# Hybrid attention/Mamba layer on one core: index queries of three token blocks instead of four, and four products for the decay sums instead of fifteen

## The chip, the core and the metric

The kernel runs on one core of a Trainium2 chip. That core has a matrix engine (TensorE, PE in the profile, with its weight loads shown apart as PEld), VectorE (DVE), ScalarE (ACT), GpSimd (POOL) and SyncE (SP), which issues most transfers. The metric is the device time of one execution in microseconds; the kernel before takes 1356.84 us, the median of three runs (1355.81 to 1357.34).

## The reference

One layer is computed for 512 new tokens of one stream (positions 0 to 511, no past) and for 64 tokens of another (positions 512 to 575, with 512 cached keys). Width 1024, everything float32. Cut to what bears on the change:

```python
h = rms_normalize(x) * g_norm_mix * (1.0 + sc1) + sh1
q, k, v, qi, ki, wi, z, xbc, dt, gate_logits = split(h @ w_in)
qi = rope(qi.reshape(b, t, 8, 64), pos); ki = rope(ki, pos)        # index queries, index keys
# per block of 128 queries:
logits = einsum('thd,sd->ths', qi, ki) * 64 ** -0.5
score = einsum('th,ths->ts', wi, relu(logits))
limit = (pos // 64 + 1) * 64
score = where(kpos < limit, score, -inf)
_, idx = top_k(score, k)            # k = 128 for the 512 tokens, 144 for the 64 (of 576 keys)
valid = idx < limit                 # keys past the limit count for nothing
o = softmax(q . k[idx]) @ v[idx]    # 16 heads, 4 key/value heads
# Mamba-2 branch:
dtp = softplus(dt + dt_bias)                      # 32 heads
acs = cumsum(dtp * -exp(a_log)) within a chunk
decay = exp(where(causal, acs_i - acs_j, -inf))   # chunked scan of xs, bm, cm
y = ssd_scan(...) + d_skip * xs, gated by silu(z), group norm
# merge of both branches by sigmoid gates, output projection, residual, SwiGLU FFN
```

The first 128 tokens of the prompt have at most 128 keys before their limit, so the top 128 are all of them: which keys such a query may read follows from its position alone.

## The kernel before, in words

**The order.** The program records every operation of every engine on paper (class `Plan`, one `Op` each) and then makes one list of all of them (`order`): it simulates the engines with a table of costs and latencies, lets the engine that can start earliest go next, and takes on that engine, of the operations that the simulation holds ready, the one recorded first (`R.prio(n)` lets an operation count as recorded n places earlier; `R.slack` holds a product back by so many us in the simulation). `emit` (line 544) then issues them, so every instruction in the trace carries L544, and groups are told apart by the names of their tiles. Any change of what is recorded makes this list anew, for the whole program.

**Products.** Weights come from HBM as `raw` tiles of 1024 columns; ScalarE rounds them to `wh`, VectorE makes the remainder `wl`. The layer's normed input stands transposed as `hTh` + `hTl` (and `hsS` for the 64 tokens). Each exact product is three: high with high, high with low, low with high. Two pools of PSUM accumulators matter: `mm`, two slots of two banks, for the wide products, and `px` and `py`, two banks each, for transposes, scores and sums.

**Stages.** (1) The input's norm and the small columns (`misc`: index keys, head weights, dt). (2) The index queries `qi`, in two halves of 256 columns (4 heads each): `tm` makes token-major products for four blocks of 128 tokens and for the 64 tokens, into `mm`; ScalarE moves them to `tok`, `rope` rotates them (two products into `tmpb` on VectorE, one on GpSimd, a sum on VectorE), and `q_stack` transposes them on PE and splits them into `qis` (high on ScalarE, low on VectorE). (3) The decay sums: from `dA` (5 chunks x 32 heads) the running sum in a chunk (`tri`), the total (`ones`), and the running sum with heads on rows, which goes through `acsT` to DRAM (`acs_d`). They are products of float32 operands. (4) Scores of blocks 4 (the 64 tokens), 1, 2, 3 and the choice of the top keys by `max` and `match_replace` on VectorE; the results are `mask1` to `mask4`. `mask0` is set by its position alone. (5) Attention for each of the four key/value heads `kv`: score products into `py`, `lg` on VectorE, `P` by ScalarE's exponential, then for each tile of 128 keys a transpose into `px`, a copy `pth` on ScalarE, the remainder `ptl` on VectorE, and two products with the values `vst` into `py`; `otmp` (ScalarE) moves out half of the sum. Two `pth` and two `ptl` buffers alternate. (6) The scan: inputs `xc` from `mm` by ScalarE, convolution `cu`, chunks that load their decay sums as `bc`. (7) Merge and FFN.

**Fillers.** 32 blocks of 128 gate columns are independent of attention and are used as work for PE between its dependent steps. A table says after which stage each block is recorded (`FILL = [5, 5, 5, 4]` for the four `kv`, 1 each for two places in the scan, 11 ahead of attention); the planner takes them when nothing recorded earlier is ready. The scan's input products (`mm<-hTh,wh` and so on, 128x288) are recorded behind attention's last `kv` and serve the same way. Their weights are split in the order of the table. `R.close(at2, ap_)` ends attention's buffers; the scan's tiles come after it.

## Time and profile before

| | before |
|---|---|
| median of three runs | 1356.84 us (1355.81 to 1357.34) |
| the profiled execution's own time | not listed apart; its span is 1353.9 us |
| PE busy | 1341.1 us of the span |
| VectorE busy | 1138.9 us |
| ScalarE busy | 756.7 us |
| GpSimd busy | 247.9 us |
| stages, read from the trace | queries and sums 60 to 125 us, top keys to 239, attention 243 to 452, scan from 452, FFN from about 950 |

A row of the profile names the line, the engine, the operation and its output and input tiles with the shape (partitions x elements), "x4" for four instructions, and in brackets how long the engine was idle just before and which instruction released it. PE's matmuls overlap, so the time from one start to the next says more than the duration of one. The trace of a product with two float32 operands shows two records for one product.

### The profile page before, as it was taken

How to read it: one execution, taken by the hardware profiler on the slowest of the kernel's cores; microseconds unless marked ns; L12 is line 12 of the kernel's file. 1: busy time of each engine (PE TensorE's matmuls, PEld its weight loads, DVE VectorE, ACT ScalarE, POOL GpSimd, SP SyncE). 2: the span in 40 equal slices, each digit the busy share in tenths (PEclk: the TensorE clock that was granted, in tenths of full speed). 3: DMA queues.
4: the chain of work that ended last, by engine and by line, in shares of the span. 5: the costliest groups of instructions: out<-in, count | busy, mean ns of one | idle time of the engine just before them, and what ended most of it. 6: DMA issues, size and time to landing. Idle time of an engine off the chain costs nothing.

```text
span 1353.9 us, 27909 instructions
## 1 busy us (share of the span) xinstructions
PE 1341.1 (99%) x10677; PEld 1307.3 (97%) x10677; DVE 1138.9 (84%) x2303; ACT 756.7 (56%) x1597; POOL 247.9 (18%) x381
## 2 busy tenths in 40 slices
PE   8999999999999999999999999999999999999998
PEld 6999999999999999999999999999999999999998
DVE  5788999887777788888887688867799999878997
ACT  5445343787777666666565342225576666665453
POOL 2312011230301234545463300002100000000000
PEclk9999999999999999999999999999999999999999
DMA  9762435574754464454445688747533343324352
GB/s 300 228 182 82 112 107 155 126 184 108 170 139 119 139 177 112 116 151 129 133 122 172 216 290 256 232 139 250 153 94 94 99 129 102 94 78 138 98 163 64
DMA packets 268454, 201.35 MB, mean 149 GB/s; under 512 B 25553, under 2 KB 239681, under 8 KB 268321
## 3 DMA queue, kind: packets, MB, share of 16 engines
q1 hardware_dynamic: 263056, 183.40, 46.2%
q0 software_dynamic: 4976, 16.05, 5.9%
q8 instruction: 83, 1.36, 0.4%
q14 instruction: 51, 0.41, 0.1%
q10 hardware_dynamic: 288, 0.13, 0.0%
HBM read 157.75 MB, written 28.96 MB: 138 GB/s over the span
## 4 chain that ended last, share of the span: by engine, by line
PE 93%; DVE 4%; issue 1%; ACT 1%; DMA 0%; POOL 0%; DVEq 0%; POOLq 0%; ACTq 0%
PE mm L544 64%; PE py L544 17%; PE px L544 12%; DVE score L544 1%; DVE m L544 1%; DVE wl L544 0%; DMA B<-in_w_down 0%; DVE tok L544 0%; DVE xs L544 0%; DVE rr L544 0%; ACT wh L544 0%; ACT wl L544 0%; POOL tok L544 0%; DVE xn L544 0%; DVE kst L544 0%
## 5 line engine op out<-in xcount | busy, mean ns | idle before, releaser
L544 ACT ACTIVATE wh<-raw 128x1024 fp32r<-128x1024 f32 (+3 forms) x144 | 140.5, 979 | 170.5 <-PE mm L544 133.0
L544 PE MATMUL mm<-hTl,wh 128*128 128x288 f32 (+1 forms) x1024 | 232.7, 302 | 0.9 <-DVE hTl L544 0.9
L544 PE MATMUL mm<-hTh,wh 128*128 128x288 f32 (+1 forms) x1024 | 231.6, 303 | 0.6 <-ACT wh L544 0.5
L544 PE MATMUL mm<-hTh,wl 128*128 128x288 f32 (+1 forms) x1024 | 230.3, 302 | 0.0
L544 PEld LDWEIGHTS mm<-hTl,wh 128*128 128x128 f32 (+1 forms) x1024 | 166.9, 189 | 3.7 <-DVE hTl L544 1.4
L544 PEld LDWEIGHTS mm<-hTh,wh 128*128 128x128 f32 (+1 forms) x1024 | 166.0, 189 | 4.0 <-ACT hTh L544 1.0
L544 PEld LDWEIGHTS mm<-hTh,wl 128*128 128x128 f32 (+1 forms) x1024 | 165.8, 189 | 1.8 <-issue 0.7
L544 DVE TENSOR_TENSOR wl<-raw,wh 128x1024 fp32r<-128x1024 f32 (+2 forms) x99 | 120.9, 1223 | 25.5 <-ACT wh L544 24.3
L544 POOL DMA_DIRECT2D wl<-raw x24 | 22.1, 919 | 472.2 <-PE px L544 313.8
L544 DVE SCALAR_TENSOR_TENSOR cu<-xc,wc,cu 128x579 f32<-128x579 f32 x96 | 83.8, 873 | 2.0 <-ACT cu L544 1.0
L544 PE MATMUL mm<-wh,hTl 128*128 128x256 f32 x256 | 73.2, 286 | 0.0
L544 PE MATMUL mm<-wl,hTh 128*128 128x256 f32 x256 | 72.5, 284 | 0.0
L544 PE MATMUL mm<-wh,hTh 128*128 128x256 f32 x256 | 72.4, 285 | 0.0
L544 DVE SCALAR_TENSOR_TENSOR aacc<-adr,sil,aacc 128x512 f32<-128x512 f32 x84 | 59.1, 753 | 5.0 <-DMA adr<-in_w_ada 4.7
L544 PE MATMUL mm<-yh,wl 128*128 128x288 f32 x256 | 55.2, 296 | 0.0
L544 PE MATMUL mm<-yh,wh 128*128 128x288 f32 x256 | 55.0, 296 | 0.0
L544 PE MATMUL mm<-yl,wh 128*128 128x288 f32 x256 | 54.9, 296 | 0.0
L544 PE MATMUL mm<-xhS,wh 128*128 128x290 f32 (+1 forms) x248 | 54.8, 296 | 0.0
L544 ACT ACTIVATE P<-lg,mn 128x128 f32<-128x128 f32 (+4 forms) x72 | 41.7, 580 | 23.1 <-DVE mn L544 22.0
L544 PE MATMUL mm<-xhS,wl 128*128 128x290 f32 (+1 forms) x232 | 51.2, 296 | 0.0
L544 ACT ACTIVATE dec<-dec,nacs 128x128 f32<-128x128 f32 x128 | 42.4, 392 | 14.4 <-POOL dec L544 14.4
L544 PEld LDWEIGHTS mm<-wh,hTl 128*128 128x128 f32 x256 | 48.3, 189 | 0.4
(569 smaller groups left out, 4077.9 us busy)
## 6 DMA issues: line engine op xcount, KB each, us to landing
raw<-in_w_in SPq DMA_DIRECT2D x80, 512.0 KB, 4.2
adr<-in_w_ada SPq DMA_DIRECT2D x36, 512.0 KB, 5.5
raw<-in_w_gate_up SPq DMA_DIRECT2D x22, 512.0 KB, 3.8
wl<-raw POOLq DMA_DIRECT2D x21, 512.0 KB, 4.9
rawu<-in_w_gate_up SPq DMA_DIRECT2D x20, 512.0 KB, 3.8
bc<-acs_d SPq DMA_DIRECT2D x32, 256.0 KB, 3.5
raw<-in_w_branch_ssm SPq DMA_DIRECT2D x16, 512.0 KB, 4.8
gate_d<-sg SPq DMA_DIRECT2D x16, 288.0 KB, 2.4
```

Of the source, the lines that this page charges most:

```text
L544: getattr(engines[x.eng], x.fn)(*[real(a) for a in x.args], **{k: real(v) for k, v in x.kw.items()})
```

## The change

Two parts, both ahead of attention. First, `tm`, `rope` and `q_stack` take an argument `first`, the first block of tokens that they treat, and the two calls for the index queries pass 1: nothing is made for the first 128 tokens, whose columns of `qis` are read by no score. Each half issues 24 fewer products of 256 columns and 2 fewer transposes; the moves out of `mm`, the four steps of the rotation and the splits into `qis` are shorter. Second, the decay sums of the five chunks are made in one product of 160 columns with `tri`, one with `ones`, one transposed product for the first four chunks (their 4 x 32 rows side by side) and one for the fifth; `acsT` and `acs_d` take that form, are stored in two parts on SP, and the chunks' loads (`bc`) read rows 32c + 4g of it.

```diff
-    def tm(name, tiles, n, out):
+    def tm(name, tiles, n, out, first=0):
         for pr in range(2):
             ps = pmm(f"{name}p{pr}")
-            for j in range(2):
+            j0 = max(first - 2 * pr, 0)
+            for j in range(j0, 2):
...
-                act.activation(out[:, 2 * pr:2 * pr + 2, :], ps[:, :, :n], AF.Copy)
+                act.activation(out[:, 2 * pr + j0:2 * pr + 2, :], ps[:, j0:, :n], AF.Copy)
...
-    def rope(name, x, tab, h, rms):
-        x4 = x.rearrange("p t (h d) -> p t h d", h=h)
-        b = ap_.tile([P, 5, h, HD], F32, name=name + "rb", tag="tmpb", bufs=1)
+    def rope(name, x, tab, h, rms, first=0):
+        x4 = x.rearrange("p t (h d) -> p t h d", h=h)[:, first:]
+        tab = tab[:, first:]
+        nb = 5 - first
+        b = ap_.tile([P, 5, h, HD], F32, name=name + "rb", tag="tmpb", bufs=1)[:, first:]
...
-    def q_stack(st, name, x, pair, h0, n_h):
+    def q_stack(st, name, x, pair, h0, n_h, first=0):
...
-        for tb in range(4):
+        f0 = P * first
+        for tb in range(first, 4):
             pe.transpose(p[:, tb * P:(tb + 1) * P], x[:, tb, P * pair:P * pair + P], ident)
...
-            for src, c0, n in ((p, (h0 + i) * NP_, NP_), (p2, n_h * NP_ + (h0 + i) * NS, NS)):
+            for src, c0, n in ((p[:, f0:], (h0 + i) * NP_ + f0, NP_ - f0), (p2, n_h * NP_ + (h0 + i) * NS, NS)):
...
-        tm(f"qi{hf}", getw(), 256, x)
-        ropes.append(rope(f"qi{hf}", x, cs2, 4, False))
+        tm(f"qi{hf}", getw(), 256, x, 1)
+        ropes.append(rope(f"qi{hf}", x, cs2, 4, False, 1))
         for pr in range(2):
-            q_stack(qis, f"qis{hf}{pr}", x, pr, 4 * hf + 2 * pr, 8)
+            q_stack(qis, f"qis{hf}{pr}", x, pr, 4 * hf + 2 * pr, 8, 1)
...
-    for c in range(5):
-        pe.matmul(p[:, 32 * c:32 * c + 32], tri, dA[:, c, :], start=True, stop=True)
-        pe.matmul(p2[:, 32 * c:32 * c + 32], ones, dA[:, c, :], start=True, stop=True)
+    pe.matmul(p[:, :160], tri, fl(dA), start=True, stop=True)
+    pe.matmul(p2[:, :160], ones, fl(dA), start=True, stop=True)
...
-    p = [px("pacsTa"), px("pacsTb", "py")]
-    for c in range(5):
-        o, i0 = (p[0][:32, P * c:P * c + P], P) if c < 4 else (p[1][:32, :NS], NS)
-        pe.matmul(o, dA[:i0, c, :], tri[:i0, :i0], start=True, stop=True)
+    p = px("pacsT")
+    pe.matmul(p[:, 0:P], fl(dA)[:, 0:P], tri, start=True, stop=True)
+    pe.matmul(p[:32, P:P + NS], dA[:NS, 4, :], tri[:NS, :NS], start=True, stop=True)
...
-    acs_d = R.dram([32, T], F32, name="acs_d")
-    sync.dma_start(acs_d, acsT)
+    acs_d = R.dram([160, P], F32, name="acs_d")
+    sync.dma_start(acs_d[0:P], acsT[:, 0:P])
+    sync.dma_start(acs_d[P:160, 0:NS], acsT[:32, P:])
...
-        sync.dma_start(bc[:, :, :L], acs_d[4 * g:4 * g + 4, i0:i0 + L][None].to_broadcast([P, 4, L]))
+        sync.dma_start(bc[:, :, :L], acs_d[32 * c + 4 * g:32 * c + 4 * g + 4, 0:L][None].to_broadcast([P, 4, L]))
```

The list of operations is made anew, and moves in places far from these lines. Three of them follow. On PE, the end of attention: the last tiles of keys of the last head group before (`ident,P` is a transpose of probabilities, `pth,vst` and `ptl,vst` the products with the values, `mm` a product of the fillers or of the scan's inputs):

```order
L544 MATMUL py_111<-ptl_2725,vst_2708 128x512
L544 MATMUL px_113<-ident_70,P_2720 128x128
L544 MATMUL px_113<-ident_70,P_2721 128x128
L544 MATMUL px_113<-ident_70,P_2722 128x128
L544 MATMUL mm_114<-hTh_126,wl_104 128x288
L544 MATMUL mm_114<-hTh_126,wh_101 128x288 x2
L544 MATMUL mm_114<-hTl_127,wh_101 128x288 x2
L544 MATMUL mm_114<-hTh_126,wl_104 128x288 x2
L544 MATMUL mm_114<-hTh_126,wh_101 128x288 x2
L544 MATMUL mm_114<-hTl_127,wh_101 128x288
L544 MATMUL py_111<-pth_2724,vst_2708 128x512
```

and the same place in the new order:

```order
L544 MATMUL px_112<-ident_70,P_2724 128x128
L544 MATMUL px_113<-ident_70,P_2721 128x128
L544 MATMUL px_113<-ident_70,P_2722 128x128
L544 MATMUL px_113<-ident_70,P_2723 128x128
L544 MATMUL px_113<-ident_70,P_2724 128x128
L544 MATMUL py_110<-pth_2725,vst_2710 128x512
L544 MATMUL py_110<-ptl_2727,vst_2710 128x512
L544 MATMUL py_110<-pth_2726,vst_2710 128x512
L544 MATMUL py_110<-ptl_2728,vst_2710 128x512
L544 MATMUL mm_115<-hTh_126,wh_102 128x288 x2
```

The ten `mm` products between the last transposes and their use have gone from there. On ScalarE, the same place before (`xc` are the scan's inputs, moved out of the `mm` slots):

```order
L544 ACTIVATE pth_2724<-px_113 128x512
L544 ACTIVATE pth_2723<-px_112 128x512
L544 ACTIVATE pth_2724<-px_113 128x512
L544 ACTIVATE otmp_2727<-py_111 64x512
L544 ACTIVATE xc_5110<-mm_115 128x288
L544 ACTIVATE xc_5110<-mm_115 128x224
L544 ACTIVATE xc_5110<-mm_115 128x64
L544 ACTIVATE cu_5112<-xc_5110,bconv_79,wc_78 128x579
L544 ACTIVATE wh_101<-raw_100 128x1024
```

and now:

```order
L544 ACTIVATE pth_2726<-px_113 128x512
L544 ACTIVATE pth_2725<-px_112 128x512
L544 ACTIVATE pth_2726<-px_113 128x512
L544 ACTIVATE otmp_2729<-py_110 64x512
L544 ACTIVATE xc_5056<-mm_115 128x288
L544 ACTIVATE xc_5056<-mm_115 128x224
L544 ACTIVATE xc_5056<-mm_115 128x64
L544 ACTIVATE xc_5057<-mm_114 128x288
L544 ACTIVATE xc_5057<-mm_114 128x224
```

Both `mm` slots now hold inputs of the scan when attention ends; before, one did. On PE, the transposes of the first half's rotated index queries stood among the products of the 64 tokens (hsS):

```order
L544 MATMUL mm_114<-wl_106,hsS_128 128x256
L544 MATMUL mm_114<-wh_101,hsS_128 128x256
L544 MATMUL mm_114<-wl_104,hsS_128 128x256
L544 MATMUL py_110<-ident_70,tok_682 128x128
L544 MATMUL px_113<-ident_70,tok_682 128x128 x4
L544 MATMUL mm_114<-wh_101,hsS_128 128x256
```

and in the new order stand among products with hTh and hTl, 39 rows nearer to the program's start:

```order
L544 MATMUL mm_115<-wh_102,hTh_126 128x256
L544 MATMUL mm_115<-wl_105,hTh_126 128x256
L544 MATMUL mm_115<-wh_102,hTl_127 128x256
L544 MATMUL py_110<-ident_70,tok_682 128x128
L544 MATMUL px_113<-ident_70,tok_682 128x128 x3
L544 MATMUL mm_115<-wh_102,hTh_126 128x256
```

The 39 rows are counted from the first instruction of PE.

More of the change, by code (lines that the diff above doesn't have):

```diff
@@ L1022, in rope @@
             vec.tensor_tensor(x4, x4, r[:, :, :, None].to_broadcast([P, 5, h, HD]), OP.mult)
-        vec.tensor_tensor(b[..., 0:32], x4[..., 32:64], tab[:, :, None, 64:96].to_broadcast([P, 5, h, 32]), OP.mult)
-        vec.tensor_tensor(b[..., 32:64], x4[..., 0:32], tab[:, :, None, 96:128].to_broadcast([P, 5, h, 32]), OP.mult)
-        pool.tensor_tensor(x4, x4, tab[:, :, None, 0:64].to_broadcast([P, 5, h, HD]), OP.mult)
+        vec.tensor_tensor(b[..., 0:32], x4[..., 32:64], tab[:, :, None, 64:96].to_broadcast([P, nb, h, 32]), OP.mult)
+        vec.tensor_tensor(b[..., 32:64], x4[..., 0:32], tab[:, :, None, 96:128].to_broadcast([P, nb, h, 32]), OP.mult)
+        pool.tensor_tensor(x4, x4, tab[:, :, None, 0:64].to_broadcast([P, nb, h, HD]), OP.mult)
         return vec.tensor_tensor(x4, x4, b, OP.add)
@@ L1175, in build @@
     vec.tensor_tensor(wst, wst, dtp, OP.mult)
-    p = [px("pacsTa"), px("pacsTb", "py")]
-    for c in range(5):
-        o, i0 = (p[0][:32, P * c:P * c + P], P) if c < 4 else (p[1][:32, :NS], NS)
-        pe.matmul(o, dA[:i0, c, :], tri[:i0, :i0], start=True, stop=True)
+    p = px("pacsT")
+    pe.matmul(p[:, 0:P], fl(dA)[:, 0:P], tri, start=True, stop=True)
+    pe.matmul(p[:32, P:P + NS], dA[:NS, 4, :], tri[:NS, :NS], start=True, stop=True)
     R.slack = SLACK
-    acsT = ix.tile([32, T], F32, name="acsT")
+    acsT = ix.tile([P, P + NS], F32, name="acsT")
     with R.prio(4000):
-        act.activation(acsT[:, :NP_], p[0][:32, :], AF.Copy)
-        act.activation(acsT[:, NP_:], p[1][:32, :NS], AF.Copy)
-    acs_d = R.dram([32, T], F32, name="acs_d")
-    sync.dma_start(acs_d, acsT)
+        act.activation(acsT[:, 0:P], p[:, 0:P], AF.Copy)
+        act.activation(acsT[:32, P:], p[:32, P:P + NS], AF.Copy)
+    acs_d = R.dram([160, P], F32, name="acs_d")
+    sync.dma_start(acs_d[0:P], acsT[:, 0:P])
+    sync.dma_start(acs_d[P:160, 0:NS], acsT[:32, P:])
     with R.after([ropes[0]]):
```

## The prediction

> **What bounds the kernel now.** I read the busy shares on the page first, then the busy time by stage, then single rows of the stage that changes.
>
> ```profile
> span 1353.9 us, 27909 instructions
> PE 1341.1 (99%) x10677; PEld 1307.3 (97%) x10677; DVE 1138.9 (84%) x2303; ACT 756.7 (56%) x1597; POOL 247.9 (18%) x381
> PE 93%; DVE 4%; issue 1%; ACT 1%; DMA 0%; POOL 0%; DVEq 0%; POOLq 0%; ACTq 0%
> ```
>
> TensorE (PE) is idle for only 1353.9 - 1341.1 = 12.8 us, and 93% of the chain that ended last is PE. The stages, each a row of window, length, busy time and count of PE, PEld (weight loads), DVE, ACT and POOL, then PE's granted clock, the DMA share and GB/s:
>
> ```profile
> 0.00:60.00 60.00, 53.07 (x566) 46.69 (x567) 38.42 (x85) 30.65 (x54) 19.76 (x39) 0.97 0.96 283
> 130.00:235.00 105.00, 104.94 (x789) 104.01 (x788) 100.34 (x233) 38.48 (x55) 9.33 (x8) 1.00 0.42 115
> 235.00:243.00 8.00, 7.09 (x53) 6.45 (x52) 6.88 (x15) 6.00 (x14) 4.60 (x6) 1.00 0.84 210
> 430.00:455.00 25.00, 25.00 (x175) 23.64 (x174) 18.20 (x43) 15.22 (x33) 0.46 (x4) 1.00 0.22 62
> 455.00:1354.00 899.00, 894.68 (x7123) 878.17 (x7122) 772.35 (x1440) 497.16 (x1079) 162.89 (x280) 1.00 0.50 147
> ```
>
> Start (6.9 us idle) and everything after 455 us (4.3 us) hold nearly all the idle time. From 130 to 235 us, while VectorE picks the top keys, VectorE is full too (100.34 of 105). So a product taken from PE is worth its whole issue time, as long as PE finds other work to take its place: the question is whether the new order still has some.
>
> **The change part by part.** First what PE no longer does.
>
> ```profile
> 66.02 15.15 PE mm L544 x128
> 81.01 0.27 PE L544 MATMUL py<-ident,tok 128*128 128x128 f32 x1
> 81.11 0.60 PE L544 MATMUL px<-ident,tok 128*128 128x128 f32 x4
> 111.74 1.20 PE L544 MATMUL px<-e,tri 128*128 128x32 f32 x10
> 104.30 1.06 PE L544 MATMUL px<-tri,e 128*32 128x128 f32 x8
> 108.89 0.30 PE L544 MATMUL py<-tri,e 64*32 64x64 f32 x2
> L544 PE MATMUL px<-tri,e x8: 272/273/297, 104.3 to 105.1; 128*32 128x128 f32 x8
> L544 PE MATMUL py<-xw,bt x64: 377/379/483, 480.7 to 769.9; 128*128 128x256 f32 x64
> ```
>
> *Query columns.* 2 halves x 8 k x 3 = 48 products of 256 columns go. 128 of them took 15.15 us, 118 ns each (products overlap, so start-to-start counts, not the 280 ns of one): 48 x 0.118 = 5.7 us. Four transposes go: (0.60 - 0.27) / 3 = 0.11 us each, 0.4 us.
>
> *Decay sums.* A product of f32 operands shows as two records. Ten 32-column ones: (1.20 - 0.28) / 9 = 0.103 us a record, 0.21 a product, 2.1 us. Four of 128 columns: (1.06 - 0.30) / 7 = 0.109, 0.22 a product, 0.9 us. The last is 0.15. Together 3.1 us. What replaces them: a 128-column one, 0.22, a 64-column one, 0.15, and two of 160 columns, a size that the trace does not show. Its bounds: not under the 128-column 0.22, not over 256 columns, whose record lasts 379 against 273 ns, so 0.22 + 2 x 0.106 = 0.43. By columns it lies a quarter of the way: 0.27. New sum 0.9 us, saving 2.2 us (1.9 to 2.3).
>
> PE sum: 5.7 + 0.4 + 2.2 = **8.3 us less**, bounds 8.0 to 8.6.
>
> *VectorE, ScalarE, GpSimd.* Eight query splits shrink from 512 to 384 columns, the rope's four multiplications and two additions from 1280 to 1024 elements: by the rows 690, 818 and 1488 ns, a quarter or a fifth less each, 1.4 + 0.65 + 0.6 = 2.6 us of VectorE. A reduction (1.49) also falls behind the last mask. None of it is on the path; it only makes the masks earlier, and the two waits here may go:
>
> ```profile
> L544 DVE TENSOR_TENSOR tmpb<-tok,cs x4: 814/818/828, 71.7 to 88.7; 128x640 f32<-128x640 f32 x4
> L544 DVE TENSOR_TENSOR tok<-tok,tmpb x6: 1481/1488/1492, 79.1 to 363.2; 128x1280 f32<-128x1280 f32 x6
> L544 DVE TENSOR_TENSOR qis<-px,qis x8: 683/690/695, 86.6 to 108.3; 64x512 fp32r<-64x512 f32 x8
> 235.99 0.44 PE L544 MATMUL py<-ident,tok 128*128 128x128 f32 x2 [0.67 <-DVE tok L544]
> 241.77 0.66 PE L544 MATMUL px<-ident,tok 128*128 128x128 f32 x4 [0.24 <-DVE kst L544]
> ```
>
> That is up to 0.9 us (0.67 and 0.24) of the 235 to 243 stage. Nothing there or between 60 and 130 us is new in kind, so small new waits are as likely; I take 0.4 us gained, between -1 and +1. The second store of the sums on SP, and SP's queue behind it, cost nothing: the first load of them (bc) is 345 us later.
>
> ```profile
> L544 SPq DMA_DIRECT2D acs_d<-acsT x1: 337/337/337, 109.5 to 109.5; - x1
> L544 SPq DMA_DIRECT2D bc<-acs_d x40: 359/360/996, 454.3 to 747.9; - x40
> ```
>
> *Where the order moves.* The planner makes the whole order anew. With 8.3 us less PE work under the same VectorE work, it pulls query and branch products ("fillers") forward: before the first attention product stand 206 instead of 196 query products of each kind (30 more in all, while 48 were removed earlier: so its start hardly moves). The fillers are a fixed stock. They lie between a transpose of probabilities, ScalarE's copy (pth), VectorE's remainder (ptl) and PE's use of both. In the new order all other key tiles keep about 1.35 us or more of PE work over those steps; the last four of the last head group have 0.44 to 0.68 us, with no filler. After the last scores there were 54 filler products in the old order (54 x 0.133 = 7.2 us, by the row of 162 below), and there are 21 now. Both PSUM slots of the wide products are then full of scan inputs, which ScalarE may move out only when attention has ended.
>
> ```profile
> 439.68 0.69 DVE L544 CUSTOM_DVE_ANT_0 lg<-py,mask 128x512 f32<-128x512 f32 x1
> 441.57 1.68 DVE L544 TENSOR_SCALAR P<-P,sm 128x512 f32<-128x512 f32 x4
> 447.90 1.29 DVE L544 TENSOR_TENSOR ptl<-px,pth 128x512 fp32r<-128x512 f32 x2
> 450.14 0.60 ACT L544 ACTIVATE pth<-px 128x512 fp32r<-128x512 f32 x1 [2.70 <-PE px L544]
> 450.77 0.69 DVE L544 TENSOR_TENSOR ptl<-px,pth 128x512 fp32r<-128x512 f32 x1 [1.58 <-ACT pth L544]
> 451.92 0.40 PE L544 MATMUL py<-ptl,vst 128*128 128x512 f32 x1
> 452.35 0.59 ACT L544 ACTIVATE otmp<-py 64x512 f32<-64x512 f32 x1 [1.61 <-PE py L544]
> 452.37 0.10 POOL L544 MEMSET xc<- 128x3 f32 x1 [33.99 <-PE py L544]
> 452.97 0.78 ACT L544 ACTIVATE xc<-mm 128x288 f32<-128x288 f32 x3
> 452.31 21.60 PE mm L544 x162
> 444.65 1.06 ACT L544 ACTIVATE wh<-raw 128x1024 fp32r<-128x1024 f32 x1
> 445.89 1.22 DVE L544 TENSOR_TENSOR wl<-raw,wh 128x1024 fp32r<-128x1024 f32 x1 [0.45 <-PE mm L544]
> ```
>
> Before, PE went through this end without a gap: 451.92, then fillers at once. Now, one wait after the other, PE's free time being what its own rows between do not fill (a 512-column product issues in 0.23 us, a transpose in 0.11, a handoff is about 0.05):
> - The remainder of the last-but-one unit's second tile stands on VectorE behind four normalisations (1.68) that need the last exponential; PE's fillers end about 1.1 us too soon: **1.1**.
> - otmp stands ahead of pth on ScalarE and starts when the unit before has ended: 0.40 + 0.05 + 0.59 + 0.60 + 0.05 = 1.7, less 0.23 + 6 transposes (0.66): **0.8**; then ptl, 0.69 + 0.06: **0.75**.
> - Third and fourth tile: pth for the third, **0.45** (0.27 + 0.05 + 0.60 less four transposes), its ptl **0.5**, the fourth's **0.1**, the rest overlapping.
> - The scan's first free slot: 0.17 until the last product ends, otmp 0.59, xc 0.78, handoffs 0.1: **1.65**. Queued behind this wait are 144 filler and scan products, then all of the scan.
>
> Sum 5.35 us. Its bounds: the slot's 1.65 with half of the rest, 3.5; and four tiles wholly in series (each 0.31 + 0.60 + 0.69 + 0.06 less 0.44, 4.9), with 1.1 and 1.65, 7.7. I take 5.3, because the two probability buffers that make the rest overlap are there in the rows (two copies in 1.09, two remainders in 1.29).
>
> **Sum.** 8.3 + 0.4 - 5.3 = 3.4 us less: the profiled span of 1353.9 becomes 1350.5. The median of the runs, 1356.84, is 2.9 us above that span, which I leave as it is: **1353.4 us**, and 1351.6 to 1355.8 with the end's bounds of 3.5 and 7.7 and the other terms held.
>
> **The rivals.** *The whole gain arrives* (the end of attention is covered after all): 1356.84 - 8.7 = 1348.1; with the waits half hidden, 1356.84 - 8.7 + 2.7 = 1350.8. For it: PE's idle time in the trace between 60 and 455 us is under 2 us, and ScalarE is busy for only 15.22 of 25 us at 430 to 455. Against it: the fillers are missing from the order, whatever the durations. *The end eats it all*: the four tiles in series and no help at 235 us: 1356.84 - 8.3 + 7.7 = 1356.2. For it: VectorE and ScalarE have split work (wl 1.22, wh 1.06) queued between the tiles; against it, the two buffers.
>
> *Slower than before*: the rope is late.
>
> ```profile
> 79.08 1.48 DVE L544 TENSOR_TENSOR tok<-tok,tmpb 128x1280 f32<-128x1280 f32 x1
> 95.42 0.33 PE L544 MATMUL py<-ident,tok 128*128 128x128 f32 x1 [0.22 <-DVE tok L544]
> ```
>
> The sum of the first half ends at 79.08 + 1.48 = 80.56, and PE's transposes of it start at 81.01, only 0.45 us later; in the second half PE already waits 0.22. In the new order these transposes stand 39 rows (first half) and 55 rows (second) nearer to the start, 4.6 and 6.5 us at 118 ns a row. If the chain behind them (ScalarE's copy, VectorE's and GpSimd's products, the sum) kept its times, PE would be there at 81.01 - 4.6 = 76.4 and wait 80.56 - 76.4 = 4.2 us, in order, with every query product behind it; as much in the second half gives 1353.4 + 8.4 = 1361.8. It makes the kernel slower once the two waits pass 1356.84 - 1353.4 = 3.4 us together. Against it: the last product of each half, which starts the chain, moves forward too (24 and 48 rows, 2.8 and 5.7 us), and the chain's three VectorE steps are 0.16 + 0.16 + 0.3 = 0.6 us shorter a half.
>
> *The clock falls at attention's end.* In every stage above that lost no time PE's clock was granted in full; in the first it was 0.97. There it was low over stretches with short waits only:
>
> ```profile
> 22.00:26.00 4.00, 2.78 (x19) 1.68 (x21) 4.00 (x7) 2.81 (x5) 1.41 (x1) 0.94 1.10 349
> 26.00:40.00 14.00, 13.35 (x186) 11.05 (x181) 7.71 (x20) 5.10 (x9) 0.00 (x0) 0.89 1.12 341
> 23.87 0.51 PE L544 MATMUL mm<-hTl,wh 128*104 128x288 f32 x2 [0.61 <-DVE hTl L544]
> ```
>
> That cost 0.06 x 4 + 0.11 x 14 = 1.8 us. If the waits at the end of attention, which are longer than this 0.61, did the same to the products behind them, the time is 1353.4 + 1.8 = 1355.2. For it: these rows; against it: the stage at 235 to 243 lost 0.9 us to waits at a clock of 1.00. [...]
>
> **How the numbers follow.** Forecast 0.5, whole gain 0.2, all eaten 0.14, clock 0.06, slower 0.1. A change under 0.2% (2.7 us, 1354.1) cannot be told from none here. About 0.7 of the forecast's cases (1351.6 to 1355.8) lie below 1354.1: faster 0.35 + 0.2 = 0.55; no change 0.15 + 0.14 + 0.06 = 0.35; slower 0.1. The range reaches down to 1348.6, which leaves out half of the whole gain (0.1), and up to 1357.0, which leaves out the late rope (0.1).
>
> **What the changed profile would show.** 60 to 130 us: the same products in less time, PE still full. About 435 to 455 us: PE idle for some 5 us, with py waiting for pth and ptl, and mm for xc. If PE is full there, the whole-gain rival was right. If PE waits for tok at 75 to 95 us, the rope was. If the idle time after 455 us grows past 4.3 us, the scan's new order costs, and I missed it.

## The result, and the profile after

The changed kernel takes 1363.74 us (median of six runs, 1360.13 to 1367.44) against 1357.03 us for the kernel before: a ratio of 1.0053 (95% interval 1.0041 to 1.0064). It is 0.5% slower. I had forecast 1353.4 us, in a range of 1348.6 to 1357.0, and gave slower a chance of 0.1. The rows below are from an execution of 1365.39 us: in them the loss is 9.8 us, in the medians 6.7.

The page of the changed kernel, its span, busy times and chain by engine:

```profile
span 1363.7 us, 27771 instructions
PE 1339.7 (98%) x10603; PEld 1301.6 (95%) x10603; DVE 1142.9 (84%) x2303; ACT 754.0 (55%) x1597; POOL 252.9 (19%) x381
PE 82%; DMA 5%; DVE 5%; ACT 4%; issue 3%; POOL 1%; SPq 0%; DVEq 0%; POOLq 0%; ACTq 0%
```

PE has 74 records fewer (10677 - 10603), as the change says: 48 products, 4 transposes, 22 records of decay sums. But it is busy for only 1.4 us less where I had 8.3, and idle for 1363.7 - 1339.7 = 24.0 us where it was 12.8. The span grows by 9.8 us: 11.2 us of new idle time less 1.4. Against the sum of the prediction, 6.9 us of busy time that should have gone are still there.

To see where, I count what PE has left to do. The same number of records left, counted from the end, is the same work left, to about 1 us (products differ in length: 0.118 us from start to start with 256 columns, 0.23 with 512). First four windows of the kernel after (length, busy time and count of each engine, PE's granted clock, DMA share, GB/s):

```profile
0.00:240.00 240.00, 230.18 (x1945) 220.74 (x1946) 200.47 (x417) 101.78 (x174) 44.39 (x58) 0.99 0.60 171
60.00:440.00 380.00, 373.11 (x2825) 362.34 (x2825) 317.79 (x747) 214.80 (x439) 64.00 (x59) 1.00 0.53 136
440.00:1364.00 924.00, 913.66 (x7223) 893.18 (x7222) 787.12 (x1474) 508.41 (x1105) 169.54 (x284) 1.00 0.49 144
462.00:1364.00 902.00, 895.08 (x7117) 877.48 (x7115) 770.78 (x1439) 494.67 (x1074) 169.07 (x280) 1.00 0.50 146
```

and three of the kernel before:

```profile
0.00:240.00 240.00, 232.07 (x1973) 222.76 (x1974) 203.30 (x422) 103.54 (x180) 44.25 (x57) 0.99 0.59 167
60.00:440.00 380.00, 378.36 (x2889) 368.31 (x2887) 319.08 (x761) 220.74 (x450) 64.76 (x59) 1.00 0.53 134
440.00:1354.00 914.00, 909.68 (x7228) 892.31 (x7226) 781.42 (x1458) 505.27 (x1095) 163.36 (x284) 1.00 0.50 146
```

At 240 us 10603 - 1945 = 8658 records are left, before 10677 - 1973 = 8704: the new kernel is 46 records ahead, some 6 us at 0.135 us a record (200 us for 1481 of them). At 440 us 7223 are left against 7228: 0.7 us ahead. At 462 us 7117 are left, which the kernel before had at about 455.8 us (7123 at 455, in the row of the prediction): 6.2 us behind. At the end it is 9.8 us behind.

| stage | after against before at its end | lost in the stage | forecast for the stage |
|---|---|---|---|
| to 240 us | 6 us ahead | 2.7 of the 8.7 us that should be there | 0 (0.4 gained) |
| 240 to 440 | 0.7 ahead | 5.5 | 0 |
| 440 to 462 (end of attention) | 6.2 behind | 6.9 | 5.3 |
| scan and FFN | 9.8 behind | 3.6 | 0 |

With each record weighted by the usual time from start to start of its kind, in place of 0.135 us for all, the four losses come out as 2.1, 6.1, 6.1 and 3.7 us (against the 8.2 us that the removed records weigh), so a cell of this table holds to about 0.8 us. Of the first one, 0.9 us stand before 60 us (559 records there, 566 before) and belong to this execution: experiments 6 and 7 keep the order of the change up to 240 us and are 7.6 and 7.3 us ahead there.

PE's waits after 60 us and up to 440 us that are longer than half a microsecond (in brackets how long PE was idle before, and for whom):

```profile
90.29 0.33 PE L544 MATMUL py<-ident,tok 128*128 128x128 f32 x1 [0.54 <-DVE tok L544]
96.16 0.39 PE L544 MATMUL mm<-wl,hTh 128*128 128x256 f32 x1 [1.07 <-DVE wl L544]
238.98 0.44 PE L544 MATMUL py<-ident,tok 128*128 128x128 f32 x2 [0.92 <-DVE tok L544]
271.21 0.39 PE L544 MATMUL py<-pth,vst 128*128 128x256 f32 x1 [0.70 <-ACT pth L544]
284.40 0.77 PE L544 MATMUL px<-ident,P 128*128 128x128 f32 x4 [1.74 <-DVE P L544]
378.37 0.44 PE L544 MATMUL px<-ident,P 128*128 128x128 f32 x2 [1.18 <-DVE P L544]
```

These are 6.15 us. And the end of attention, where the prediction had put the waits:

```profile
450.64 0.50 PE L544 MATMUL py<-ptl,vst 128*128 128x512 f32 x1 [0.32 <-DVE ptl L544]
453.13 0.49 PE L544 MATMUL py<-pth,vst 128*128 128x512 f32 x1 [0.65 <-ACT pth L544]
454.12 0.50 PE L544 MATMUL py<-ptl,vst 128*128 128x512 f32 x1 [0.49 <-DVE ptl L544]
456.20 0.49 PE L544 MATMUL py<-pth,vst 128*128 128x512 f32 x1 [0.25 <-ACT pth L544]
456.93 0.50 PE L544 MATMUL py<-ptl,vst 128*128 128x512 f32 x1 [0.23 <-DVE ptl L544]
459.51 0.85 PE L544 MATMUL mm<-hTh,wh 128*128 128x288 f32 x2 [1.48 <-ACT xc L544]
```

They are the tiles, the releasers and the order of the forecast, and 3.4 us in sum. A second cost stands behind the waits. Windows of the kernel after, behind the wait at 284.40 and the one at 459.51:

```profile
285.00:286.00 1.00, 1.00 (x8) 0.99 (x6) 1.00 (x5) 0.00 (x0) 0.00 (x0) 0.56 0.76 152
286.00:288.00 2.00, 2.00 (x8) 1.81 (x8) 1.96 (x3) 1.97 (x6) 0.00 (x0) 0.50 0.53 186
288.00:289.00 1.00, 1.00 (x7) 0.90 (x6) 0.94 (x3) 0.73 (x3) 0.00 (x0) 0.73 0.00 0
459.00:460.00 1.00, 0.49 (x2) 0.49 (x3) 0.52 (x2) 0.83 (x5) 0.23 (x2) 0.60 0.00 0
460.00:462.00 2.00, 2.00 (x10) 2.00 (x10) 0.80 (x2) 1.93 (x5) 0.00 (x0) 0.50 0.86 295
462.00:463.00 1.00, 1.00 (x8) 1.00 (x7) 1.00 (x3) 0.00 (x0) 0.00 (x0) 0.69 1.01 168
```

The granted clock is 0.50 for 3.4 us each time (0.44 + 2 x 0.50 + 0.27 = 1.71 us lost; 0.40 + 1.0 + 0.31 = 1.71, of which 0.15 fell on the last 0.31 us of the wait and cost nothing). That is 3.3 us of the 6.9 us of busy time. What is left, 3.6 us, stays open. A first product after a wait doesn't overlap one before it (the one of 512 columns at 453.13 us lasts 0.49 us, where in an unbroken row the next one starts after 0.23), and PE has 17 waits of 0.2 us or more after 60 us, 12 more than before: 0.3 us for each of these would make it up. But experiment 1 has five more than before and only 0.6 us over its removed work. Part of the clock's share belongs to the execution: the six runs range over 7 us, the kernel before's over 2 us, and the run with the mean clock at 1.000 took 1360.13 us, the ones at 0.996 and 0.997 took 1364.98 to 1367.44.

At the scan, one new wait. PE and the loads behind it in the kernel after (SPq is SyncE's queue issuing a load, decS the decay of the short chunk):

```profile
659.18 0.38 SPq L544 DMA_DIRECT2D raw<-in_w_in  x1
659.66 0.53 SPq L544 DMA_DIRECT2D bc<-acs_d  x1
665.21 0.51 POOL L544 TENSOR_SCALAR_AFFINE_SELECT decS<-bc 64x256 f32<-64x256 f32 x1 [5.59 <-DMA bc<-acs_d]
669.17 0.70 PE L544 MATMUL py<-xw,bt 128*128 128x256 f32 x2 [1.59 <-DVE xw L544]
```

and before:

```profile
648.44 0.95 SPq L544 DMA_DIRECT2D bc<-acs_d  x2
652.93 0.74 POOL L544 TENSOR_SCALAR_AFFINE_SELECT decS<-bc 64x256 f32<-64x256 f32 x1 [1.14 <-DMA bc<-acs_d]
```

The small load now stands behind a weight load of 512 KB: from issue to use 5.55 us (659.66 to 665.21), before 4.5 at most (648.44 to 652.93). The new form of the stored sums is not the reason: the queries alone (experiment 3) have the old form, and there too the load stands behind a weight load, takes 5.5 us (658.96 to 664.43) and PE waits:

```profile
668.30 0.70 PE L544 MATMUL py<-xw,bt 128*128 128x256 f32 x2 [1.76 <-DVE xw L544]
```

### The profile page after: what moved, and what is told of

It is laid out like the page before. It is cut to its first block, busy times and chain, and to the rows that moved or that the text cites. A ratio compares the mean times of both kernels' runs of the same rounds, so it can differ in the third digit from the quotient of the medians.

```text
span 1363.7 us, 27771 instructions
## 1 busy us (share of the span) xinstructions
PE 1339.7 (98%) x10603; PEld 1301.6 (95%) x10603; DVE 1142.9 (84%) x2303; ACT 754.0 (55%) x1597; POOL 252.9 (19%) x381
## 4 chain that ended last, share of the span: by engine, by line
PE 82%; DMA 5%; DVE 5%; ACT 4%; issue 3%; POOL 1%; SPq 0%; DVEq 0%; POOLq 0%; ACTq 0%
PE mm L544 56%; PE py L544 15%; PE px L544 11%; DMA raw<-in_w_in 2%; DMA wl<-raw 1%; ACT wh L544 1%; DMA adr<-in_w_ada 1%; DMA bc<-acs_d 1%; DVE wl L544 1%; ACT wl L544 1%; DVE aacc L544 0%; ACT dec L544 0%; POOL tok L544 0%; DMA stage<-o_d 0%; DVE tok L544 0%
## 5 line engine op out<-in xcount | busy, mean ns | idle before, releaser
L544 PE MATMUL mm<-wl,hTh 128*128 128x256 f32 x240 | 67.8, 284 | 1.1 <-DVE wl L544 1.1
L544 PE MATMUL mm<-wh,hTl 128*128 128x256 f32 x240 | 68.1, 285 | 0.0
L544 PE MATMUL mm<-wh,hTh 128*128 128x256 f32 x240 | 66.9, 283 | 0.0
L544 PEld LDWEIGHTS mm<-wl,hTh 128*128 128x128 f32 x240 | 45.1, 188 | 1.4 <-DVE wl L544 1.3
```

The source lines that it names most:

```text
L544: getattr(engines[x.eng], x.fn)(*[real(a) for a in x.args], **{k: real(v) for k, v in x.kw.items()})
```

## The experiments

The working theory after the result was that the removed work is worth what the prediction says, and that the new order of the whole program costs more than it. To hold one and vary the other, each operation got a field `real`: the planner plans with the full operation, and a reduced one (or none) is issued in its place: `cut(op, ...)` names what is issued for `op`, and `cut(op)` alone leaves it out. Where the work is called reduced, the index queries that no score reads are not made; nothing else is left out in any run.

**1. The change's work in the order of before (e1).** The products and transposes of the first token block and eleven of the fifteen sums are planned and not issued; the rest is issued at its reduced size.

```diff
-            getattr(engines[x.eng], x.fn)(*[real(a) for a in x.args], ...)
+            for fn, args, kw in [(x.fn, x.args, x.kw)] if x.real is None else x.real:
+                getattr(engines[x.eng], fn)(*[real(a) for a in args], ...)
...
+                            if tb < first:
+                                cut(o)          # planned, not issued
```

> The change with the order of the kernel before: the planner still plans with the full work, and the instructions that the change removes are left out of the finished list, the others are shortened, so that only the removed rows differ. Theory A (the new order is to blame): the 8.3 us of TensorE work come off, since each key tile of attention keeps the fillers that it had; VectorE's chain of scores and top keys starts earlier by what its own queue allows (it is busy 46 of the 52 us before it), so 1349 to 1352, a full clock from 40 us on and no wait of over 1 us between 245 and 470 us. Rival B (the removed work lay beside VectorE's chain and was worth nothing): the top-key chain starts no earlier, TensorE waits some 8 us for the last mask at 230 to 245 us, and the time is within 1355 to 1358.

Measured: 1353.42 us, ratio 0.9983 (0.9974 to 0.9992). Faster than before, by about 2 us, and between the two theories. PE is busy for 1333.4 us, 7.7 less than before, so the size of the removed work was right (8.3 forecast); but 5.5 us of it came back as idle time. From this run, the window in which it appears (4.97 us idle, before 0.28), and PE's two longest waits with the VectorE and GpSimd rows ahead of the second:

```profile
60.00:130.00 70.00, 65.03 (x542) 62.69 (x541) 60.72 (x103) 30.15 (x65) 12.92 (x7) 1.00 0.51 141
102.68 0.55 PE L546 MATMUL px<-ident,tok 128*128 128x128 f32 x3 [1.11 <-DVE qis L546]
108.64 3.12 DVE L546 TENSOR_SCALAR score<-lg,wi 128x288 f32<-128x288 f32 x1
108.66 2.94 POOL L546 TENSOR_TENSOR kx<-kx,tabs 128x1280 f32<-128x1280 f32 x1 [3.57 <-ACT lg L546]
112.53 0.81 PE L546 MATMUL py<-kis,qis 128*128 128x288 f32 x4 [1.46 <-DVE wst L546]
```

In the old order PE reaches each of these places sooner and waits there for VectorE. What arrives at the first product of attention (248.25 us before, 245.99 now) is 2.3 us, and that is what arrives at the end. So the loss of the change is not in its work; but the removed work is not worth 8.3 us in the old order either.

**2. The work of before in the order of the change (e5).** The converse: the products of the first token block, the full sizes and the fifteen sums are issued at the places of the new order.

```diff
+                            if j0 and j == j0:   # the first block's product with the second's
+                                cut(o, ("matmul", (ps[:, 0, :n], l[:, k, 0:P], w[:, a, :]), kw), (o.fn, o.args, o.kw))
```

> The mirror of the first experiment: the order that the planner makes of the change, but with the whole work of the kernel before (the 48 products, four transposes and eleven small products stand beside those that are left, the other steps have their old size). Theory A' (the loss is the new order, whatever the work): 1353.9 plus some 8 to 12 us, 1362 to 1368, as slow as the change or slower by up to 3 us. Rival F (the order is good for the work that it was made for, and the loss comes of work that is too small to cover VectorE's chain): with the work back, attention starts no later and the stock lasts, so 1355 to 1359.

Measured: 1372.28 us, ratio 1.0114 (1.0101 to 1.0127), slower than both theories had it. With the two kernels and experiment 1 the table is complete (medians):

| | order of before | order of the change |
|---|---|---|
| full work | 1355.5 to 1357.0 | 1372.28 |
| reduced work | 1353.42 | 1363.74 |

In the new order the removed work is worth 8.5 us, in the old one about 2. The new order costs 16 us with the full work and 10 with the reduced. That the order costs is shown (the full work may suffer more in an order that was planned for less); what in it costs is the question of the rest.

**3. Each part alone, planned anew (e3, e4).** The queries without the sums, and the sums without the queries; the other part as before.

```diff
-        tm(f"qi{hf}", getw(), 256, x, 1)
+        tm(f"qi{hf}", getw(), 256, x)      # sums alone; so for rope and q_stack
```

> The first part of the change alone (index queries of the first block not made), decay sums as before. Theory A (stock of fillers): 6.1 us less TensorE work ahead of VectorE's chain means about as many fillers eaten early, so attention's end waits nearly as in the whole change: 1359 to 1365. Rival D (the decay sums' new form is to blame, by its loads and its place in VectorE's queue): this part alone is faster than before, 1350 to 1353.

> The second part alone (four products for the decay sums, new form of the stored sums), index queries as before. Theory A: 2.2 us less TensorE work, so a third of the loss at most: 1356 to 1359. Rival D (the sums' new form is to blame): 1361 to 1365, with waits in the scan for the products with xw as in the whole change.

Measured: queries alone 1368.24 us, 1.0089 (1.0076 to 1.0103); sums alone 1365.16 us, 1.0068 (1.0055 to 1.0080). The queries alone are worse than both together, and the sums alone, which take only 2.2 us from PE, lose 0.7%. A loss in proportion to the work removed (less work, so fillers used up sooner) is out as the whole cause. The sums alone come within 0.2 us of the range that was given to their new form as the cause, but experiment 4 issues that form in the old order without a loss.

**4. Each part alone in the old order (e10, e11).** As experiment 1, with one part.

> Only the first part of the change (index queries), in the old order. If the 6.1 us of TensorE work lie ahead of chains that VectorE and GpSimd set, they come back as waits for tok, qis and the first score step but for 1 to 2.5 us: 1353.5 to 1355.3. If they were worth their issue time there: 1350 to 1351.

> Only the second part (decay sums), in the old order: 2.2 us less TensorE work at 101 to 113 us, just ahead of the first score. If VectorE sets the start of the scores, next to nothing: 1355.5 to 1356.5. If TensorE's work there counts: 1353.5 to 1354.5. The scan's loads in their new form are in it too: if they cost something, it is slower than before.

Measured: queries 1354.05 us, 0.9984 (0.9975 to 0.9992); sums 1355.01 us, 0.9990 (0.9981 to 0.9999). In the old order neither harms. The two gains, 0.16% and 0.10%, make 0.26% against 0.17% for both together, which the intervals can't tell apart. PE's idle time from 60 to 130 us does add up: 2.84 us for the queries, 2.31 for the sums, 4.97 for both, where it was 0.28 before.

**5. One more block for the end of attention (e2).** The forecast named the missing fillers at the end; one gate block is moved there from the scan.

```diff
-    FILL = [5, 5, 5, 4]
-    MID = 1
+    FILL = [5, 5, 5, 5]
+    MID = 0
```

> The change as it is, but one of the 32 filler blocks (48 products, 6.4 us) that stood in the scan (MID) is recorded with attention's last head group, so attention's stock is one block larger; what is computed is the same. Theory A (attention has run out of fillers because TensorE ate 8 us of them while it waited for VectorE's top keys): the waits at 270 to 285, 378 and 450 to 460 us go, with them both stretches at half clock; 9.8 us of the longer span go and the gain shows: 1348 to 1353. Rival C (the new order as such is bad, in the index stage and the scan too): only the 5 us of attention's last waits and 1.7 us of the last slow stretch go, 1355 to 1358, and the scan, one block poorer, loses some of that.

Measured: 1362.0 us, 1.0048 (1.0034 to 1.0062), the same as the change within the intervals. The waits at the end are gone, as this row of the run shows, but from there to the end of the span PE is idle for 1362.3 - 462 - 889.87 = 10.4 us, 3.8 more than in the change (1363.7 - 462 - 895.08 = 6.6). Neither theory's time came:

```profile
440.00:462.00 22.00, 22.00 (x156) 20.86 (x155) 16.28 (x38) 13.00 (x30) 0.47 (x4) 1.00 0.30 86
462.00:1363.00 901.00, 889.87 (x7064) 870.32 (x7062) 777.36 (x1437) 495.44 (x1074) 179.43 (x280) 1.00 0.49 145
```

The stock is one: what one stage gets, the scan lacks.

**6. GpSimd out from under the softmax (e7).** At the wait of 284.40 in the change VectorE normalises four tiles of P beside a product of the query rotation on GpSimd. Here that product (`q2`) is issued on VectorE, ahead of the sum that uses it.

```diff
+        if name == "q2":
+            o.real, s.real = [], [(o.fn, o.args, o.kw), (s.fn, s.args, s.kw)]
```

> The change with one product moved: the third product of the rotation of head group 2's queries, which GpSimd makes in 2.91 us at 281 us, is made by VectorE (1.5 us) just before the sum. Theory (GpSimd's product holds VectorE's normalisation of P, which took 2.62 us instead of 0.42, and through it TensorE, 1.74 us at 284 us, which brings the stretch of half clock at 285 us): wait and slow stretch go, 1.5 to 3.4 us less than the change: 1360 to 1362. Rival (VectorE is full there, and its added 1.5 us costs TensorE as much): the wait stays within 0.7 us of what it was, and so does the time.

Measured: 1359.78 us, 1.0030 (1.0018 to 1.0043), some 3 us better than the change (the two intervals just touch). The rows of the change:

```profile
281.22 2.91 POOL L544 TENSOR_TENSOR tok<-tok,tabs 128x1280 f32<-128x1280 f32 x1 [1.88 <-DVE sm L544]
281.73 3.61 DVE L544 TENSOR_SCALAR P<-P,sm 128x384 f32<-128x384 f32 x4
```

and of the experiment:

```profile
280.42 1.40 DVE L546 TENSOR_SCALAR P<-P,sm 128x384 f32<-128x384 f32 x4
287.24 0.50 PE L546 MATMUL py<-ptl,vst 128*128 128x512 f32 x1 [1.00 <-DVE ptl L546]
```

The four steps take 1.40 us without the GpSimd product beside them and 3.61 with it. The first of them begins 0.5 us after GpSimd's product, lasts 2.62 us and ends 0.2 us after it; the other three last 0.41 us. Why the first lasts until GpSimd's product ends, the rows don't show. A wait of 1.00 appears behind, but by the count of records the change is 7.2 us ahead of the kernel before at 270 us and 2.4 at 290 us, and this kernel 7.6 and 5.9. So GpSimd's product cost some 3 us of what was lost between 240 and 440: 1.74 us of wait, the low clock behind it (0.50 for 3.4 us, 1.71 us lost), and the refill, less the new wait of 1.00.

**7. The load ahead of the weights (e6).** The weight load ahead of the late `bc` on SP is put behind it; nothing else moves.

```diff
+        i = next(k for k, x in enumerate(seq) if ... == "s5_4bc")     # the load of the short chunk
+        j = max(k for k in range(i) if ... seq[k].eng == "sync")      # the weight load ahead of it
+        seq.insert(i, seq.pop(j))
```

> The change with one pair of transfers on SP exchanged: in the scan of the sixth group the planner has put a load of weights (raw, 512 KB) ahead of the load of the last chunk's decay sums (bc); here the small load goes first. All other rows stay. Theory (the small load's 5.6 us to landing, and with it TensorE's wait of 1.59 us for xw at 669 us, come of the queue): that wait goes, 1.5 to 2 us less than the change: 1361 to 1362.5. Rival (the load is slow by its new form, 256-byte pieces at 512-byte steps): the wait stays, no difference.

Measured: 1359.99 us, 1.0030 (1.0019 to 1.0041). The wait falls from 1.59 to 0.54 us:

```profile
663.08 0.70 PE L548 MATMUL py<-xw,bt 128*128 128x256 f32 x2 [0.54 <-DVE xw L548]
```

So that wait comes of the queue. But the median falls by more than this wait, and with the records weighted by kind PE loses the same 1.9 to 2.0 us between 660 and 675 us in both kernels. What the median gained comes from elsewhere; the mean clock of the profiled execution is 0.998, where that of the change is 0.996. The edit is repeated in experiment 11, where it gains nothing.

**8. The old order, GpSimd's products on VectorE (e8, e12).** On top of experiment 1, the rotation products of both index-query halves and of the attention keys (`k`); then that of the keys alone.

```diff
+        if name == "k":      # first run: name in ("qi0", "qi1", "k")
+            cut(o[2])
+            cut(o[3], (o[2].fn, o[2].args, o[2].kw), (o[3].fn, o[3].args, o[3].kw))
```

> The first experiment's kernel (change in the old order) with the third product of the rotations of the index queries and of the keys on VectorE in place of GpSimd. In the old order VectorE's first score step stood still for 2.75 us beside GpSimd's product of the keys, and a step of the decay sums 2.13 us. Theory (these stalls, not VectorE's own work, hold the chain of top keys): VectorE pays 1.2 + 1.2 + 1.5 us and saves 2.75 + 2.13, the chains get shorter by GpSimd's 2.4 to 2.9 us, TensorE's waits at 78, 93 and 112 us shrink, the last mask comes 1 to 2 us earlier: 1351 to 1353. Rival (VectorE's full queue is the bound): 1354 to 1357.

> The first experiment's kernel with one product, the third of the keys' rotation, on VectorE (1.5 us) in place of GpSimd (2.9 us at 108.7 us, beside which VectorE's first score step took 3.12 us instead of 0.37). The index queries' rotations stay on GpSimd. Theory (a stall of 2.75 us for a product of 1.5): the last mask comes about 1.2 us earlier and TensorE's wait of 1.46 us at 112.5 goes: 1351.5 to 1352.8. Rival (VectorE's total to the last mask counts and the stall overlapped a wait for TensorE's scores anyway): 1353 to 1354.5.

Measured: all three 1353.77 us, 0.9979 (0.9971 to 0.9988), no gain over experiment 1; the keys alone 1351.15 us, 0.9961 (0.9947 to 0.9974), the lowest median of all runs, 2.3 us under experiment 1; the intervals of these two meet at 0.9974, and the profiled execution, of 1353.31 us, has the span of experiment 1's (1351.6 and 1351.7 us), so this gain is not as sure as the rows. The keys-alone run, at the place of the 3.12 us above:

```profile
109.54 0.37 DVE L546 TENSOR_SCALAR score<-lg,wi 128x288 f32<-128x288 f32 x1
111.47 1.49 DVE L546 TENSOR_TENSOR kx<-kx,tabs 128x1280 f32<-128x1280 f32 x1
```

The score step takes 0.37 us instead of 3.12, the product 1.49 on VectorE instead of 2.94 on GpSimd, and PE's wait of 1.46 for `wst` is gone. With the query halves moved too, VectorE has four fifths of 1.49, 1.2 us, more ahead of each of their sums, and PE waits 2.1 us for the first half's `tok`, where it waited 0.83 in experiment 1.

**9. Three microseconds more on VectorE, ahead of the scores (e9).** On top of experiment 1, both 128x640 products of the key rotation are issued three times, which changes no value.

```diff
+        if name == "k":
+            for u in o[:2]:
+                cut(u, *3 * [(u.fn, u.args, u.kw)])
```

> The first experiment's kernel (change in the old order) with 3.1 us more on VectorE ahead of the first score step: the two products of the keys' rotation (0.78 us each) are made three times over, with the same result. Nothing else moves. Theory (VectorE's queue ahead of the scores sets the start of attention, and a late start is paid in TensorE's waits there): first score and last mask come 3 us later, TensorE waits as much more at 108 to 118 or 230 to 250 us, and the time is 2.5 to 3.5 us longer than the first experiment's, 1356 to 1357. Rival (VectorE has slack there, some 7 of 54 us idle, and the chain takes it up): within 0.8 us of the first experiment, 1353 to 1354.2.

Measured: 1355.17 us, 0.9991 (0.9983 to 1.0000); the interval overlaps that of experiment 1. Attention starts at 246.79 us, 0.8 later than there. So VectorE's row ahead of the scores sets the start only in part: of 3.1 us added, 0.8 arrived there, and the median lies between the two theories. Neither "VectorE alone is the bound there" nor "it has room" is borne out.

**10. The totals in the bank of the running sums (e13).** In the change, scores come slowly. PE's products of the totals (`ones`) and of the first scores (`kis,qis`), and VectorE's step that frees the totals, in the kernel after:

```profile
96.97 0.43 PE L544 MATMUL py<-e,ones 128*128 128x160 f32 x2
110.44 0.43 PE L544 MATMUL py<-kis,qis 128*128 128x288 f32 x2
113.54 0.43 PE L544 MATMUL py<-kis,qis 128*128 128x288 f32 x2
119.03 0.32 DVE L544 TENSOR_TENSOR wst<-py,nacs 128x160 f32<-128x160 f32 x1
```

The totals stand in one of the two `py` banks for 22 us (before for 12, from 101.50 to 113.33 us), and meanwhile the scores have one. The order of PE's products showed it before the run; I had not looked there. Before:

```order
L544 MATMUL py_110<-kis_701,qis_702 128x288 x2
L544 MATMUL py_111<-kis_701,qis_702 128x288 x2
...
L544 MATMUL py_110<-kis_701,qis_702 128x288 x2
L544 MATMUL py_111<-kis_701,qis_702 128x288 x2
```

and in the new order, where the other bank comes in only with the sixth pair (the sums alone, experiment 3, show the same rows):

```order
L544 MATMUL py_111<-kis_701,qis_702 128x288 x2
...
L544 MATMUL py_111<-kis_701,qis_702 128x288 x2
L544 MATMUL px_112<-e_0_703,tri_72 128x160
...
L544 MATMUL py_111<-kis_701,qis_702 128x256 x2
...
L544 MATMUL py_110<-kis_701,qis_702 128x288 x2
```

The edit lets the totals lie beside the running sums, and the list is planned anew:

```diff
-    p2 = px("ptot", "py")
+    p2 = p[:, 256:]
```

> The change, with the totals of the decay sums (ones) written into the bank of the running sums (px) in place of a py bank of their own, and the order made anew. In the trace of the change the totals stand in py from 96.97 us until VectorE reads them at 119.03, since the running sums that VectorE needs with them come only at 117.89; the scores of the 64 tokens, whose two halves alternate between the two py banks, go through one bank, and the first max comes at 134.0 us in place of 125.3. Theory (that held bank is what delays attention in the new order): scores in pairs, first max at 118 to 126 us, first attention product at 245 to 248 us in place of 250.95, and 2.5 to 6 us less than the change: 1357.5 to 1361. Rival (attention's start does not matter, the fillers are eaten either way, and what counts is the shortage at attention's end): the start moves and the waits at 250 to 460 us grow by as much, 1362 to 1365.

Measured: 1358.92 us, 1.0021 (1.0012 to 1.0029), 4 us better than the change. Scores alternate again, and the first `max` of the key choice stands at 121.93 us (change 134.01, before 125.30); the first product of attention at 244.95 (250.95, 248.25). Between 240 and 440 us this kernel loses 0.8 us by the count of records (0.3 weighted by kind), where the change lost 5.5 (6.1). Since the list was planned anew, this doesn't prove that the bank alone did it: the GpSimd product under the softmax has moved as well.

**11. What is left, undone one at a time (e14, e15, e16).** On top of experiment 10: the rotation products of `k` and `q2` on VectorE; or one more block with the last head group, taken from ahead of attention, so that the stock for the scan stays (`FILL = [5, 5, 5, 5]`, 10 ahead instead of 11); or that and the load of experiment 7.

```diff
-    FILL = [5, 5, 5, 4]
+    FILL = [5, 5, 5, 5]
```

> The same, and the third product of the rotation of the keys and of head group 2's queries on VectorE in place of GpSimd, without a new order. If the held bank and GpSimd's products beside VectorE are together the larger part of the new order's cost: 1351 to 1357, as fast as the change in the old order. If the shortage of fillers at attention's end remains the larger part: 1357 to 1362.

> The kernel of e13 (totals beside the running sums) with one of the 11 filler blocks ahead of attention recorded with attention's last head group instead, so that TensorE can't eat it before; the total stock is the same. Theory (a shortage at attention's end, since fillers are taken as soon as TensorE is free): the waits of 3.5 us at 445 to 454 us and the slow stretch behind them go, 3.5 to 5.5 us less than e13: 1353.5 to 1355.5, and no new waits ahead of 440 us. Rival (the stock is too small wherever it stands): the waits move ahead, to 230 to 440 us, 1357 to 1360.

> e15 with the scan's load of weights put behind the small load of the last chunk's sums in the sixth group, as in e6. If the wait of 1.59 us for xw at 661 us comes of the queue: 1 to 1.7 us less than e15, 1352 to 1354.5. If not: the same as e15.

Measured: rotations 1361.25 us, 1.0038 (1.0024 to 1.0051), 2.3 us over experiment 10 with overlapping intervals, and 2.9 us of waits for `ptl` where that has 1.7; one block back 1352.68 us, 0.9975 (0.9966 to 0.9985), 6 us better; with the load 1352.51 us, 0.9973 (0.9962 to 0.9983), no difference. The end of attention in experiment 10 and with the block back:

```profile
440.00:462.00 22.00, 18.55 (x112) 15.63 (x111) 14.96 (x25) 12.24 (x27) 5.42 (x19) 0.92 0.42 107
440.00:462.00 22.00, 22.00 (x163) 21.59 (x162) 15.54 (x23) 14.27 (x35) 7.94 (x23) 1.00 0.66 162
```

3.5 us of idle time become none, and a clock of 0.92 becomes 1.00 (22 x 0.08 = 1.8 us). Here the scan pays little for it: from 462 us to the end the two lose 2.7 and 3.7 us by the count of records. So the prediction's end of attention was a matter of when the stock is used, as far as one edit shows it after which the list was planned anew. The repair of the load changes nothing in the time, though its wait goes from 1.59 to 0.53 us here too. Of the versions that beat both kernels, two stand out: the changed work in the old order with the keys' rotation on VectorE (0.9961), and the newly planned one with two edited lines (0.9975).

## Why the prediction was wrong, point by point

- **What the work is worth: right.** 8.3 us by the sum; 7.7 us of PE's busy time in experiment 1, 8.5 us of the median between experiment 2 and the change. (By its own terms the upper bound is 8.4, not 8.6; nothing rests on it.)
- **End of attention: right in place and releasers; the sum is near by luck.** Forecast 1.1, 0.8, 0.75, 0.45, 0.5, 0.1 and 1.65 us, 5.3 in sum; measured 6.9 (6.1 weighted): the waits are only 3.4 us, 1.9 less than forecast (the first, forecast at 1.1, is 0.32), but the low clock, which had no term in the sum, adds 1.6, and 1.9 us were not taken apart. That the waits go when a filler is held back is shown by experiments 5 and 11.
- **The step that failed** is the sentence that "all other key tiles keep about 1.35 us or more of PE work over those steps", with the zero that it put on the new order from 240 to 435 us. It is the largest of the four terms that make up the 13 us between the forecast span of 1350.5 and the measured 1363.7 (5.5 here, 3.6 in the scan, 2.7 before 240 us, 1.6 at the end of attention). It counted PE work between a transpose and its use, and took VectorE's and ScalarE's steps at the durations of the old trace. In the new order GpSimd's rotation product falls on the normalisation, which then takes 3.61 us for 1.40, and no 1.35 us of PE work covers that. 5.5 us were lost there, of which experiment 6 gave back some 3. The rest (the waits of 0.70 and 1.18 us for `pth` and `P` at 271 and 378 us) was not taken apart.
- **VectorE's savings, "none of it is on the path", and the 0.4 us at 235 us: wrong.** Of the 8.7 us, 6 are there at 240 us (7.3 to 7.6 in the executions of experiments 6 and 7). The wait at 235.99 (0.67) did not go, it is 0.92; new ones of 0.54 and 1.07 came. In the old order it is worse: PE finds nothing to take the removed work's place, and 60 to 130 us lies idle for 5 us (experiment 1). The prediction's first part had the condition, "as long as PE finds other work to take its place"; I looked at it at the end of attention alone.
- **The scan: wrong.** It had no term. 3.6 us were lost there, and the sign that the prediction named came: PE is idle for 6.6 us after 462 us, past its 4.3. One place is shown (1.59 us for a load queued behind weights), but its repair took the wait to 0.54 us and no measurable time off the kernel. Where the scan's loss comes from stays open.
- **The rivals.** *The clock falls* was held at 0.06, for the end of attention, and is what happened behind two waits: 1.6 us there and 1.7 at 285 us in the profiled run, 1.8 forecast. The clock was 0.50 for 3.4 us each time; the waits ahead of the two stretches are 1.74 and 1.48 us, and PE was busy for 1.67 and 1.76 of the 3.41 us just before each. What brought the clock down was not shown. *Slower by a late rope* is out: the first half's transposes stand at 77.41 us without a wait, the second half's wait 0.54 us (90.29), where it had 4.2 each. *Whole gain* and *end eats it all* fall with the stages ahead of the end.
- **The chances.** Slower had one mechanism with 0.1. The order of the whole program was new, and I had read three places of it; that alone should have carried more than 0.1.

## What to carry to other kernels

Where a greedy planner makes the order, a small edit is two changes: the work, and a new order for everything else. They are told apart by issuing the edited work in the old order and the old work in the new one, and here the second outweighed the first. When reading a new order before a run, look at which accumulator bank each product takes and how long its last reader leaves it occupied, at what lies on GpSimd beside each dependent VectorE step, and at what stands ahead of a small load on its queue: a count of filler products at one place tells nothing of the others.

## What the runs showed of the hardware that I had not expected

- `TENSOR_SCALAR` steps of VectorE took longer beside a GpSimd product: one of 128x288 took 3.12 us beside a product of 2.94, and 0.37 without; four of 128x384 took 3.61 beside a product of 2.91, and 1.40 without.
- PE's granted clock was 0.50 for 3.4 us at two waits of the change, of 1.74 and 1.48 us among busy stretches; experiment 2 has both waits (1.8 and 1.5 us) at a granted clock of 1.00 behind them. The six runs of the change range over 7 us, from 1360.13 us at a mean clock of 1.000 to 1367.44 at 0.997. The rows above put the starts of the two stretches at 285.12 and 459.20 us, and PE was busy for about half of the 3.41 us just before each (first number behind the comma):

```profile
281.71:285.12 3.41, 1.67 (x11) 1.10 (x10) 3.41 (x6) 0.81 (x2) 2.42 (x1) 1.00 0.30 54
455.79:459.20 3.41, 1.76 (x6) 0.67 (x4) 1.79 (x4) 1.96 (x5) 0.24 (x2) 1.00 0.00 0
```

  What sets the waits with a low clock behind them apart from those of experiment 2 was not tested.
- The product of the keys' rotation took 1.49 us on VectorE and 2.94 on GpSimd. My estimate from these rows is that moving one pays where a VectorE step beside it is the longer for it (3.12 against 0.37 us), and costs where none is. The medians of experiments 8 and 11 lie that way, with intervals that meet or overlap.
